# A fixed instruction order in the feed-forward's opening with five plain pairs, and the sample's narrow matmuls of the token mixing moved beside the prompt's

## The chip, the cores and the metric

The kernel runs on one core of one Trainium2 chip. The core has TensorE (matrix multiplies, PE in the profile; its weight loads are PEld), VectorE (DVE), ScalarE (ACT), GpSimd (POOL) and SyncE (SP), which here only issues transfers. The metric is the device time of one launch in microseconds (us), as a median of runs. The profile is one execution recorded by the hardware profiler.

## The reference, cut to what matters

One inference step of a two-layer decoder trunk of width 1024, on a prompt of 512 positions and a sample of 8 sequences with 8 new positions each (64 positions). The kernel treats them together as T = 576 columns. Each layer is:

```
x = x + norm(mixing(norm(x)))       # mixing: three groups of heads beside each other
x = x + norm(conv_ffn(norm(x)))     # d_ff = 2816
mixing: one input projection, then
   A  dilated sliding-window softmax attention, 8 heads of 64
   B  HGRN2 gated linear recurrence, 4 heads, key 128, value 64
   C  GLA linear attention, 4 heads, key 32, value 64
   and one output projection of the joined heads
conv_ffn: up projection to 2 x 2816 columns, causal depthwise convolution of width 3,
   h = gelu(a) * b of the two halves, down projection to 1024
```

The outputs are the two activations, the updated recurrent and convolution states, and the attention's key and value caches, whose old rows are copied from one place of HBM to another.

## The kernel before, in words

Everything is fp32 in value. A factor is split in two parts of a shorter fp32 format (`whi` and `wlo` of a weight, `xha`/`xm` and `xla` of an activation), and a product is the sum of three matmuls: high by high, low by high, high by low (L132 to L134). ScalarE writes the high part (L113) and VectorE the low one (L114). The 576 columns are worked in a half of 320 (the 64 of the sample and 256 of the prompt) and one of 256.

**Token mixing.** The projection's matmuls fill TensorE, and between them stand the small matmuls of the linear-attention heads. For each head and level, the scores are one matmul for the sample (L487, 64 stationary columns) and eight for the prompt (L493), in two PSUM banks. Each fp32 matmul shows in the profile as two. `ke`, the attention's probabilities `pr` and the head outputs' squares `sqs` each have a sample part that is only 64 wide (L529, L954, L721). The head norms take their inverse root on GpSimd (`rsqrt`, L250), once for the prompt's 8 columns (`rh`) and once for the sample's 2 (`rhs`).

**Feed-forward, up projection.** There are 22 pairs of tiles (a and b), j = 0 to 21; tile ui = 2j + i. The first `NPLAIN` pairs are plain: a tile is 8 x 3 matmuls for the half of 320 and 8 x 3 for that of 256 (`col_tile`), and VectorE takes the result out of PSUM into `u` (L1055). The later pairs are fast (`fast_pair`, `products`): seven products of 12 matmuls on 288 columns, a Strassen-like scheme, whose weights need four additions on VectorE and a split of sums (`weights`), and whose activations `sxh`, `sxl` are made once per layer by `combine(0)` to `combine(3)` (L1117 to L1126) on VectorE and ScalarE. These four stand behind tiles 3 to 6. After the two tiles of a pair come `conv_end` (three taps, L1075 on ScalarE, L1076 and L1077 on VectorE) and `h_tile` (gelu L1086, product L1087, split L1097 and L1098). Finished `h` go to the down projection, whose columns `c` are placed after pairs by `FF_AFTER`, in groups of pairs (group 0: pairs 0 to 3).

**What sets the order.** The engines' order in the opening is not written out: a scheduler places instructions by their readiness, with `behind(...)` as bounds. PSUM offers the plain tiles three main banks, so a tile's matmuls wait until VectorE has emptied the bank three halves earlier. SP issues all transfers from one queue in order; after each pair it issues two cache copies (`copy_cache`, 768 KB each, from HBM to HBM).

Of the kernel before, what the change touches and what calls it, by code (L numbers as in the profile page):

```python
# [8 lines left out]
F32 = mybir.dt.float32  # L9
# [30 lines left out]
FF_AFTER = ({4: 2, 5: 2, 6: 2, 7: 2}, {8: 2, 9: 2, 10: 2, 11: 2}, {12: 2, 13: 2, 14: 2, 15: 2},  # L40
# [3 lines left out]
NPLAIN = 4  # L44
COMBINE = (3, 4, 5, 6)
# [34 lines left out]
def trunk_kernel(ctx: ExitStack, tc: tile.TileContext, I, O):  # L80
# [16 lines left out]
    def s_bank():  # L97
        return bank("s", 2)
# [72 lines left out]
    mhalf = cst.tile([P, 8], F32, name="mhalf")  # L171
# [73 lines left out]
    def rsqrt(src, m, scale, name, rows=P):  # L245

        v = rs.tile([P, 8], F32, name="rv", tag="rv", bufs=2)[:rows, :m]
        r = rs.tile([P, 8], F32, name=name, tag=name, bufs=2)[:rows, :m]
# [189 lines left out]
    def gla_tile(l, hp, kq, q, k, b, heads, kd, vt, vs, vcol, s0, o_ps, os_ps, outs, qbd, j, sds, vms, kTs):  # L438
# [58 lines left out]

# [31 lines left out]
        PE.transpose(tb[:TS, :P], ke[:, 0:TS], ident)  # L529
# [56 lines left out]
    def mixing(l, act, first):  # L586
# [16 lines left out]
        with ExitStack() as mx:  # L603
# [63 lines left out]
            with ExitStack() as hx:  # L667
# [40 lines left out]
                def finish(ft):  # L708

                    o, osm = o_holder[ft]  # L710
                    sqt = hp.tile([P, TP], F32, name="sqt", tag="t512", bufs=2)
                    S.activation(sqt, o, AF.Square)
                    sqs = hp.tile([P, TP], F32, name="sqs", tag="t512", bufs=2)
                    S.activation(os_sb[:, ft, :], osm[:, :TS], AF.Copy)
                    S.activation(sqs[:, :TS], osm[:, :TS], AF.Square)
# [15 lines left out]
                    for e in range(2):  # L731
                        mm = PE.matmul(tb[64 * e:64 * e + 64, :TS], rsm[:, e:e + 1].to_broadcast([TS, 64]),
                                       ident[:TS, :TS], start=True, stop=True)
# [79 lines left out]
            G.memset(sTs[TS:, :], 0.0)  # L813
            G.memset(vas[TS:, :], 0.0)

            for p in range(4):
# [121 lines left out]
                pr = sp.tile([P, NEED + TS], F32, name="pr", tag="pr", bufs=1)  # L938
# [18 lines left out]
                V.tensor_copy(sTs[:TS, :], tb[:TS, 256:384])  # L957
# [52 lines left out]
    def ffn(l, y, xpool, act, first):  # L1010
# [20 lines left out]
        with ExitStack() as fx:  # L1031
# [6 lines left out]
            def conv_begin(ui):  # L1038
# [14 lines left out]
                def plain(b, hf, t0, n):  # L1053
                    r = R[:, t0:t0 + n]
                    place(t0, n, lambda d, c: V.tensor_tensor(d, c(b), c(r), ALU.mult))  # L1055
                    if hf:
                        conv_end(ui)
# [7 lines left out]
            def conv_end(ui):  # L1065
                u = us.pop(ui)
                uv = u[:, 0:80].rearrange("p (b t) -> p b t", t=10)
                G.tensor_copy(cso[:, ui, 0:16].rearrange("p (b t) -> p b t", t=2), uv[:, :, 8:10])
                G.tensor_copy(cso[:, ui, 16:18], u[:, NU - 2:NU])  # L1069
                c = cp.tile([P, NU - 2], F32, name="c", tag="c", bufs=2)  # L1070

                def wc(i):
                    o = PR_WC + (l * 2 * NJ + ui) * 3 + i
                    return par[:, o:o + 1]
                S.activation(c, u[:, 0:NU - 2], AF.Copy, scale=wc(0))  # L1075
                V.scalar_tensor_tensor(c, u[:, 1:NU - 1], wc(1), c, ALU.mult, ALU.add)  # L1076
                V.scalar_tensor_tensor(c, u[:, 2:NU], wc(2), c, ALU.mult, ALU.add)  # L1077
                cs[ui] = c
                if ui % 2:
                    h_tile(ui // 2)  # L1080
# [3 lines left out]
            def h_tile(j):  # L1084
                ca, cb = cs.pop(2 * j), cs.pop(2 * j + 1)
                S.activation(ca, ca, AF.Gelu_apprx_tanh)  # L1086
                V.tensor_tensor(cb, ca, cb, ALU.mult)  # L1087
# [3 lines left out]
                for hf, d0, d1, c0, c1 in ((0, 0, TS, 0, 80), (0, TS, 320, 80, 336), (1, 0, 256, 336, NU - 2)):  # L1091
                    src, dh, dl = cb[:, c0:c1], hh[j][hf][:, d0:d1], hl[j][hf][:, d0:d1]
                    if c0 == 0:
                        src = src.rearrange("p (b t) -> p b t", t=10)[:, :, 0:8]
                        dh = dh.rearrange("p (b t) -> p b t", t=8)
                        dl = dl.rearrange("p (b t) -> p b t", t=8)
                    S.activation(dh, src, AF.Copy)  # L1097
                    V.tensor_tensor(dl, src, dh.bitcast(F32), ALU.subtract)  # L1098
# [13 lines left out]
            def combine(i):  # L1112

                with behind(last_lo[0].ins):
                    x1, x2, ua, ta = (y[4 * (i % 2) + m] for m in range(4))
                    for k, d in ((i, x1), (i + HK, x2)):
                        V.scalar_tensor_tensor(d, xt[k], gnorm(l, 2, k), R, ALU.mult, ALU.mult)  # L1117
                    V.tensor_tensor(ua[:, :SH], x1[:, :SH], x1[:, SH:], ALU.subtract)
                    V.scalar_tensor_tensor(ua[:, SH:], x2[:, SH:], -1.0, ua[:, :SH], ALU.mult, ALU.subtract)
                    V.tensor_tensor(ta[:, :SH], x2[:, SH:], x1[:, SH:], ALU.subtract)  # L1120
                    V.scalar_tensor_tensor(ta[:, SH:], ua[:, SH:], -1.0, x2[:, :SH], ALU.mult, ALU.subtract)
                    hi, lo = (cp.tile([P, 7 * SH], F32R, name=f"{n}{i}", tag=f"{n}{i}") for n in ("sxh", "sxl"))
                    for src, m, n in ((x1[:, :SH], B11, 1), (x2, B21, 2), (ua, U1, 2), (ta, T3, 2)):
                        cols = slice(m * SH, (m + n) * SH)
                        S.activation(hi[:, cols], src, AF.Copy)
                        V.tensor_tensor(lo[:, cols], src, hi[:, cols].bitcast(F32), ALU.subtract)  # L1126
                    xs.append((hi, lo))

            def weights(j):
# [11 lines left out]
                w2 = split_w(ws, WN)  # L1141
                w1 = split_w(r1, WN, sw, 2)
                V.tensor_tensor(r0[:, b], r0[:, b], ws[:, a], ALU.add)
                w3 = split_w(r0[:, b], HW)
                return w0, w1, w2, w3

            def fast_pair(j):
                with behind(last_lo[0].ins if j == NPLAIN else None):
                    w0, w1, w2, w3 = weights(j)
                e1, e2 = (conv_begin(2 * j + i)[1] for i in range(2))  # L1150
                with behind(last_mm[0].ins if j == NPLAIN else None):
                    products(w0, w1, w2, w3, e1, e2)
# [32 lines left out]

            def up(j):
                if j >= NPLAIN:
                    fast_pair(j)
                else:
                    for ui in (2 * j, 2 * j + 1):  # L1190
                        if ui >= NFIRST:
                            col_tile(load_w(I["w_up"][l, ui]), xh, xl, allk, conv_begin(ui)[0])
                            if ui in COMBINE:
                                combine(COMBINE.index(ui))
                copy_cache()
                copy_cache()
# [13 lines left out]
            for j in range(NJ + 1):  # L1210
                if j < NJ:
                    up(j)
                    if j == NPLAIN - 1:

                        xpool.release()
                        sw = right_pool(f"sw{l}")
# [231 lines left out]
```

## Time and profile before

| | |
|---|---|
| median of 3 runs | 1683.43 us (1682.94 to 1683.83) |
| profiled execution, and its span | 1681.14 us, 1679.4 us |
| TensorE busy | 1606.9 us, 96% |
| VectorE, ScalarE, GpSimd busy | 1248.1, 877.6, 556.9 us |
| TensorE's granted clock, mean | 0.985 |

The busy shares are means over stages of different kinds. The two layers follow each other; in layer 0 mixing takes the time to about 443 us, the feed-forward's opening is 443 to 515 us, and layer 1 repeats it some 831 us later. The page's 40 slices show TensorE at 9 tenths nearly everywhere, with a dip at the twelfth slice (the opening of layer 0, about 462 to 504 us) and at the thirty-second (the same place of layer 1).

### The profile page before, as it was taken

Reading aid. Unit: us, or ns where it says so; the run is one execution under the profiler, and the core shown is the slowest. Engines: PE = TensorE matmul, PEld = TensorE weight load, DVE = VectorE, ACT = ScalarE, POOL = GpSimd, SP = SyncE. Lnnn points to the kernel's source line nnn. Section 1 sums busy time; section 2 is a strip of 40 time slices with the busy share of each in tenths; the row PEclk is TensorE's granted clock in tenths of the full one; section 3 lists DMA queues with packets and bytes.
Section 4 is the critical chain, followed back from the end, with each engine's and each line's share of the span. In section 5 each row is a group of like instructions: output and inputs, shape, how many; then the busy total and the mean of one; then the engine's idle time right before and its main releaser. Section 6 shows DMA issues by size and latency. Waiting matters only on the chain.

```text
span 1679.4 us, 35933 instructions
## 1 busy us (share of the span) xinstructions
PE 1606.9 (96%) x14256; PEld 1526.1 (91%) x14256; DVE 1248.1 (74%) x2472; ACT 877.6 (52%) x1638; POOL 556.9 (33%) x800
## 2 busy tenths in 40 slices
PE   8999999999979999999989999989999799999997
PEld 7888997789879999999988899968998799999997
DVE  6775765656898888888757757566568978888985
ACT  6754524564556545555456544255735555555541
POOL 4554332302542111221365553332044411212303
PEclk9999999999989999999999999999999899999999
DMA  5221326848424545653522212378474264456432
GB/s 187 71 71 59 103 100 258 298 181 313 142 102 164 212 159 171 220 200 105 174 80 84 78 65 80 120 280 336 159 272 157 82 213 157 171 200 242 149 119 104
DMA packets 74889, 270.36 MB, mean 161 GB/s; under 512 B 10689, under 2 KB 23265, under 8 KB 73185
## 3 DMA queue, kind: packets, MB, share of 16 engines
q1 hardware_dynamic: 74720, 268.07, 45.0%
q8 instruction: 112, 1.84, 0.4%
q14 instruction: 57, 0.46, 0.1%
HBM read 250.11 MB, written 85.02 MB: 200 GB/s over the span
## 4 chain that ended last, share of the span: by engine, by line
PE 76%; DVE 10%; ACT 5%; POOL 3%; issue 3%; DMA 2%; POOLq 0%; SPq 0%; ACTq 0%; DVEq 0%
PE ps_m L132 14%; PE ps_m L134 13%; PE ps_m L133 13%; PE ps_m L1164 4%; PE ps_m L1162 4%; PE ps_m L1163 4%; DVE wlo L114 2%; PE ps_t L1163 2%; PE ps_t L1164 2%; PE ps_t L1162 2%; PE ps_s L493 2%; DMA wraw<-in_w_up 1%; PE ps_o L965 1%; PE ps_o L869 1%; POOL x L352 1%
## 5 line engine op out<-in xcount | busy, mean ns | idle before, releaser
L113 ACT ACTIVATE whi<-wraw 128x1024 fp32r<-128x1024 f32 (+4 forms) x284 | 247.0, 877 | 209.2 <-PE ps_m L133 55.4
L114 DVE TENSOR_TENSOR wlo<-wraw,whi 128x1024 fp32r<-128x1024 f32 (+4 forms) x284 | 285.4, 1010 | 94.6 <-ACT whi L113 88.3
L132 PE MATMUL ps_m<-xha,whi 128*128 128x320 f32 x864 | 272.4, 316 | 5.4 <-ACT whi L113 3.1
L133 PE MATMUL ps_m<-xla,whi 128*128 128x320 f32 x864 | 270.9, 314 | 0.0
L134 PE MATMUL ps_m<-xha,wlo 128*128 128x320 f32 x864 | 268.4, 314 | 0.5 <-DVE wlo L114 0.5
L132 PE MATMUL ps_m<-xm,whi 128*128 128x256 f32 x864 | 248.6, 288 | 18.5 <-DVE u L1055 18.5
L134 PE MATMUL ps_m<-xm,wlo 128*128 128x256 f32 x864 | 247.8, 287 | 0.0
L133 PE MATMUL ps_m<-xm,whi 128*128 128x256 f32 x864 | 246.9, 286 | 0.0
L132 PEld LDWEIGHTS ps_m<-xm,whi 128*128 128x128 f32 x864 | 165.9, 192 | 22.0 <-issue 20.5
L132 PEld LDWEIGHTS ps_m<-xha,whi 128*128 128x128 f32 x864 | 164.1, 190 | 9.5 <-ACT whi L113 4.3
L1162 PE MATMUL ps_m<-sxh,whi 128*128 128x288 f32 x576 | 170.0, 296 | 0.7 <-ACT acc L1168 0.7
L1163 PE MATMUL ps_m<-sxh,wlo 128*128 128x288 f32 x576 | 169.7, 295 | 0.0
L1164 PE MATMUL ps_m<-sxl,whi 128*128 128x288 f32 x576 | 169.7, 295 | 0.0
L133 PEld LDWEIGHTS ps_m<-xm,whi 128*128 128x128 f32 x864 | 166.1, 192 | 1.5 <-issue 1.1
L134 PEld LDWEIGHTS ps_m<-xm,wlo 128*128 128x128 f32 x864 | 166.1, 192 | 1.1 <-issue 0.2
L133 PEld LDWEIGHTS ps_m<-xla,whi 128*128 128x128 f32 x864 | 164.3, 190 | 2.5 <-issue 2.0
L134 PEld LDWEIGHTS ps_m<-xha,wlo 128*128 128x128 f32 x864 | 163.3, 190 | 2.8 <-issue 1.4
L1069 POOL COPY cso<-u 128x2 f32<-128x2 f32 x88 | 74.4, 845 | 268.3 <-DVE u L1180 199.5
L1162 PEld LDWEIGHTS ps_m<-sxh,whi 128*128 128x128 f32 x576 | 108.4, 188 | 1.2 <-ACT acc L1168 1.2
L1163 PEld LDWEIGHTS ps_m<-sxh,wlo 128*128 128x128 f32 x576 | 108.7, 189 | 0.0
L1164 PEld LDWEIGHTS ps_m<-sxl,whi 128*128 128x128 f32 x576 | 108.3, 188 | 0.0
L1041 POOL COPY u<-cso 128x16 f32<-128x16 f32 x88 | 59.8, 682 | 136.7 <-DVE c L1077 86.9
(342 smaller groups left out, 4187.6 us busy)
## 6 DMA issues: line engine op xcount, KB each, us to landing
wraw<-in_w_up SPq DMA_DIRECT2D x88, 512.0 KB, 3.8
kv<-in_ck SPq DMA_DIRECT2D x32, 768.0 KB, 6.6
kv<-in_cv SPq DMA_DIRECT2D x32, 768.0 KB, 7.0
out_ck<-in_ck SPq DMA_DIRECT2D x32, 768.0 KB, 7.7
out_cv<-in_cv SPq DMA_DIRECT2D x32, 768.0 KB, 6.8
wraw<-in_w_s SPq DMA_DIRECT2D x42, 512.0 KB, 3.6
wraw<-in_w_dn SPq DMA_DIRECT2D x48, 256.0 KB, 2.6
x<-xdr SPq DMA_DIRECT2D x24, 288.0 KB, 6.4
```

Of the source, the lines that this page charges most:

```text
L113: S.activation(hi[:, :n], raw[:, :n], AF.Copy)
L114: last_lo[0] = V.tensor_tensor(lo[:, :n], raw[:, :n], hi[:, :n].bitcast(F32), ALU.subtract)
L132: PE.matmul(out, ah, bh, start=(i == 0), stop=False)
L133: PE.matmul(out, ah, bl, start=False, stop=False)
L134: last_mm[0] = PE.matmul(out, al, bh, start=False, stop=(i == n - 1))
L352: (V if dram_out and k % 4 == 3 else G).tensor_tensor(xk, xk, yk, ALU.add)
L493: mm = PE.matmul(bp[64 * hh:64 * hh + 64, cp * nh * 32:(cp + 1) * nh * 32], xk[:, c0:c0 + 64], moving(c0), start=True, stop=True)
L1041: G.tensor_copy(uv[:, :, 0:2], cso[:, ui, 0:16].rearrange("p (b t) -> p b t", t=2))
L1069: G.tensor_copy(cso[:, ui, 16:18], u[:, NU - 2:NU])
L1162: PE.matmul(b, wh, xh, start=i == 0 and not more, stop=False, skip_group_check=more)
L1163: PE.matmul(b, wl, xh, start=False, stop=False, skip_group_check=more)
L1164: PE.matmul(b, wh, xl, start=False, stop=i == HK - 1, skip_group_check=more)
```

## The change

Two independent parts.

*Token mixing.* For heads with one group (`nh == 1`) the sample's score matmul writes columns 128 to 159 of the prompt's PSUM bank, directly ahead of the prompt's eight, and its masked copy follows the prompt's. The transposes of `ke` and of `pr` for the sample take 128 columns instead of 64. `finish` squares prompt and sample into one tile and makes five sum matmuls and one inverse root of 10 columns, instead of four and one, with roots of 8 and 2. `pr` becomes a tile of the layer with a zeroed tail.

*Feed-forward's opening.* `NPLAIN` is 5 instead of 4, so pair 4 is two plain tiles. `opening()` writes out the order of VectorE, ScalarE and GpSimd for tiles 3 to 9 under `manual_schedule`: norms, combinations, low parts, taps, convolution sums, gelu, splits, evacuations (`ev`) and weights, with the weights of pair 5 made early. The column groups of the down projection's group 0 follow pairs 5, 6 and 7 (2, 3 and 3) instead of pairs 4 to 7 (2 each). Ten cache copies, which stood two after each pair, are all issued after the opening, and the two of pair 5 follow without a weight load between.

```diff
-FF_AFTER = ({4: 2, 5: 2, 6: 2, 7: 2}, ...
+FF_AFTER = ({5: 2, 6: 3, 7: 3}, ...
-NPLAIN = 4
-COMBINE = (3, 4, 5, 6)
+NPLAIN = 5
...
+            bp = s_bank()
             if sample:
-                bs = s_bank()
-                PE.matmul(bs[:TS, :nh * 32], xk[:, 0:TS], moving(0), start=True, stop=True)
-                level_scores(B, lv, sds[:TS], bs[:TS, :nh * 32])
-            bp = s_bank()
+                bs = bp[:TS, 128:160] if nh == 1 else s_bank()[:TS, :nh * 32]
+                PE.matmul(bs, xk[:, 0:TS], moving(0), start=True, stop=True)
+                if nh > 1:
+                    level_scores(B, lv, sds[:TS], bs)
...
             level_scores(B, lv, sdm, bp[:, :128 * nh])
+            if sample and nh == 1:
+                level_scores(B, lv, sds[:TS], bs)
...
-        PE.transpose(tb[:TS, :P], ke[:, 0:TS], ident)
+        PE.transpose(tb[:, :P], ke[:, 0:P], ident)
...
-                    for i in range(4):
-                        PE.matmul(tb[:, 2 * i:2 * i + 2], sqt[:, i * P:(i + 1) * P], blk2, start=True, stop=True)
-                    r = rsqrt(tb[:, :8], 8, 1.0, "rh")
-                    tb = t_bank()
-                    mark(f"f{ft}.a", PE.matmul(tb[:TS, :2], sqs[:, :TS], blk2, start=True, stop=True))
-                    rsm = rsqrt(tb[:TS, :2], 2, 1.0, "rhs", TS)
+                    for i, c0 in enumerate((0, P, 2 * P, 3 * P, T - P)):
+                        mm = PE.matmul(tb[:, 2 * i:2 * i + 2], sq[:, c0:c0 + P], blk2, start=True, stop=True)
+                    mark(f"f{ft}.a", mm)
+                    r = rsqrt(tb[:, :10], 10, 1.0, "rh")
...
-                mm = PE.transpose(tb[:TS, 256:384], pr[:, 768:832], ident)
+                mm = PE.transpose(tb[:, 256:384], prs[:, NEED:], ident)
...
+                def ev(*keys):
+                    for key in keys:
+                        if key[1] == 0:
+                            evs[key[0]] = conv_begin(key[0])[0]
+                        evs[key[0]](*bs.pop(key))
+                        if halves:
+                            mm()
...
+                with tc.manual_schedule(engines=ORDERED):
...
+                    ev((4, 0))
+                    load(6)
+                    c.append(normalize(1))
+                    combine(1, *c[1])
+                    taps(2, 3)
+                    ev((4, 1))
+                    conv_sums(2, 3)
+                    h_gelu(1)
+                    ev((5, 0))
+                    lows(1, c[1][0])
+                    load(7)
+                    ev((5, 1), (6, 0))
...
+                    ev((8, 1), (9, 0))
+                    w = weights(NPLAIN)
+                    next(w)
+                    ev((9, 1))
+                    h_split(2)
+                    early[NPLAIN] = next(w)
+                for ui in range(6, 2 * NPLAIN):
+                    conv_end(ui)
+                for _ in range(2 * NPLAIN):
+                    copy_cache()
```

VectorE's queue in layer 0 before, around the evacuation that ends the long wait; `L1055 u` is the evacuation of PSUM, `L1126 sxl` a low part of the combined activations, `L1076` and `L1077` the convolution sums, `L114 wlo` the low part of a weight, L1140 an addition for a fast weight.

```order
L1076 SCALAR_TENSOR_TENSOR c<-u,par,c 128x592
L1126 TENSOR_TENSOR sxl_6067<-y_4688,sxh_6066 128x576
L1077 SCALAR_TENSOR_TENSOR c<-u,par,c 128x592
L1120 TENSOR_TENSOR y_4690<-y_4688,y_4687 128x288
L114 TENSOR_TENSOR wlo<-wraw,whi 128x1024
L1119 SCALAR_TENSOR_TENSOR y_4689<-y_4688,y_4689 128x288
L1121 SCALAR_TENSOR_TENSOR y_4686<-y_4685,y_4684 128x288
L114 TENSOR_TENSOR wlo<-wraw,whi 128x1024
L1126 TENSOR_TENSOR sxl_5981<-y_4685,sxh_5980 128x576
L1077 SCALAR_TENSOR_TENSOR c<-u,par,c 128x592
L114 TENSOR_TENSOR wlo<-ws,whi 128x1024
L1055 TENSOR_TENSOR u<-ps_m,rbc 128x8x8
```

The same queue after, a stretch of `opening()`; `L1059 u` is now the evacuation, L1139 the norm, L1146 to L1149 the combination, L1093 the convolution sums and L1156 the low parts.

```order
L1139 SCALAR_TENSOR_TENSOR y_4649<-x_4922,par,rbc 128x576
L1146 TENSOR_TENSOR y_4650<-y_4648 128x288
L1147 TENSOR_TENSOR y_4651<-y_4649,y_4648 128x288
L1148 SCALAR_TENSOR_TENSOR y_4650<-y_4649,y_4650 128x288
L1149 SCALAR_TENSOR_TENSOR y_4651<-y_4650,y_4649 128x288
L1059 TENSOR_TENSOR u<-ps_m,rbc 128x256
L1093 SCALAR_TENSOR_TENSOR c<-u,par,c 128x592 x4
L1059 TENSOR_TENSOR u<-ps_m,rbc 128x8x8
L1059 TENSOR_TENSOR u<-ps_m,rbc 128x256
L1156 TENSOR_TENSOR sxl_5873<-y_4648,sxh_5872 128x288
L1156 TENSOR_TENSOR sxl_5873<-y_4649,sxh_5872 128x576
```

Evacuations stand at most some ten instructions apart, where twenty stood between two of them before (L1055 at places 636 and 658 of the queue).

TensorE's queue in the mixing of layer 0, before: one sample matmul (L487) alone between projection matmuls.

```order
L132 MATMUL ps_m<-xm_149,whi 128x256
L133 MATMUL ps_m<-xm_149,whi 128x256
L134 MATMUL ps_m<-xm_149,wlo 128x256
L487 MATMUL ps_s<-lev 64x32
L132 MATMUL ps_m<-xm_152,whi 128x256
L133 MATMUL ps_m<-xm_152,whi 128x256
```

After, the sample's matmul (now L488) directly ahead of the prompt's eight (now L494).

```order
L132 MATMUL ps_m<-xm_158,whi 128x256
L488 MATMUL ps_s<-lev 64x32
L494 MATMUL ps_s<-lev 64x32 x8
L488 MATMUL ps_s<-lev 64x32
L494 MATMUL ps_s<-lev 64x32 x8
L529 MATMUL ps_t<-con,ke 128x128 x4
```

No sample matmul of a single group stands alone any more; over both layers 13 did.

SP's queue of layer 0's opening before, in which pairs of copies stand between the weight loads.

```order
L120 DMA wraw<-in_w_up 128x1024 x2
L1029 DMA out_ck<-in_ck 16x12288 x2
L1134 DMA wraw<-in_w_up 128x1024 x2
L1029 DMA out_ck<-in_ck 16x12288 x2
L120 DMA wraw<-in_w_dn 128x512 x2
L1134 DMA wraw<-in_w_up 128x1024 x2
```

After, from tile 6's weights on.

```order
L119 DMA wraw<-in_w_up 128x1024 x4
L1163 DMA wraw<-in_w_up 128x1024 x2
L1033 DMA out_ck<-in_ck 16x12288 x12
L119 DMA wraw<-in_w_dn 128x512 x2
L1163 DMA wraw<-in_w_up 128x1024 x2
L1033 DMA out_ck<-in_ck 16x12288 x2
```

Twelve copies stand in one piece ahead of the first two loads of the down projection's weights (`w_dn`).

## Rows read from the trace of the kernel before

**Rows 1.** Two windows: busy us (instructions) of PE, PEld, DVE, ACT, POOL; clock; DMA.

```profile
440.00:480.00 40.00, 32.93 (x243) 32.05 (x241) 38.11 (x71) 22.84 (x34) 14.21 (x18) 0.98 0.39 139
480.00:520.00 40.00, 34.41 (x243) 33.77 (x244) 37.59 (x67) 23.39 (x48) 16.69 (x25) 0.89 0.43 151
```

**Rows 2.** TensorE's waits in the two layers' openings: total us, times, longest.

```profile
PE ps_m L132 <- DVE u L1055: 9.9, 2, 9.6
...
PE ps_m L132 <- DVE u L1055: 8.6, 1, 8.6
```

**Rows 3.** Timeline of TensorE at the stall: start, duration, instruction, [wait, releaser].

```profile
484.95 0.55 PE L132 MATMUL ps_m<-xm,whi 128*128 128x256 f32 x1 [9.58 <-DVE u L1055]
...
485.52 0.41 PE L134 MATMUL ps_m<-xm,wlo 128*128 128x256 f32 x1
485.73 0.41 PE L132 MATMUL ps_m<-xm,whi 128*128 128x256 f32 x1
```

**Rows 4.** Timeline of TensorE in the mixing: narrow matmuls alone and in company.

```profile
61.19 0.31 PE L134 MATMUL ps_m<-xha,wlo 128*128 128x320 f32 x1
61.43 0.30 PE L487 MATMUL ps_s<-lev 128*64 128x32 f32 x2
61.66 0.42 PE L132 MATMUL ps_m<-xha,whi 128*128 128x320 f32 x1
61.92 0.31 PE L133 MATMUL ps_m<-xla,whi 128*128 128x320 f32 x1
...
63.57 1.12 PE L493 MATMUL ps_s<-lev 128*64 128x32 f32 x32
...
65.12 0.27 PE L529 MATMUL ps_t<-con,ke 128*64 128x128 f32 x1
65.15 0.36 PE L133 MATMUL ps_m<-xm,whi 128*128 128x256 f32 x1
65.35 0.28 PE L134 MATMUL ps_m<-xm,wlo 128*128 128x256 f32 x1
```

**Rows 5.** Timeline of TensorE, matmuls at full pace.

```profile
601.33 0.31 PE L132 MATMUL ps_m<-xha,whi 128*128 128x320 f32 x1
601.48 0.31 PE L133 MATMUL ps_m<-xla,whi 128*128 128x320 f32 x1
601.62 0.28 PE L132 MATMUL ps_m<-xm,whi 128*128 128x256 f32 x1
601.74 0.28 PE L133 MATMUL ps_m<-xm,whi 128*128 128x256 f32 x1
```

**Rows 6.** Timeline of VectorE through the opening.

```profile
443.67 3.50 DVE L114 TENSOR_TENSOR wlo<-wraw,whi 128x1024 fp32r<-128x1024 f32 x3
...
475.57 0.68 DVE L1140 TENSOR_TENSOR ws<-wraw 128x512 f32<-128x512 f32 x1
476.17 0.82 DVE L1076 SCALAR_TENSOR_TENSOR c<-u,par,c 128x592 f32<-128x592 f32 x1
...
488.05 0.55 DVE L1055 TENSOR_TENSOR u<-ps_m,rbc 128x64 f32<-128x64 f32 x2
488.51 0.68 DVE L114 TENSOR_TENSOR wlo<-wraw,whi 128x512 fp32r<-128x512 f32 x1
...
506.35 1.23 DVE L114 TENSOR_TENSOR wlo<-wraw,whi 128x1024 fp32r<-128x1024 f32 x1 [0.16 <-ACT whi L113]
```

**Rows 7.** Timeline of ScalarE in the opening.

```profile
458.45 1.06 ACT L113 ACTIVATE whi<-wraw 128x1024 fp32r<-128x1024 f32 x1 [4.47 <-issue]
...
466.20 0.77 ACT L1075 ACTIVATE c<-u,par 128x592 f32<-128x592 f32 x1
466.88 0.67 ACT L1125 ACTIVATE sxh<-y 128x576 fp32r<-128x576 f32 x1
```

**Rows 8.** Landing of the copies issued at 446.4 and 447.0, and the load at 447.7.

```profile
DMA to landing us min/median/max: 6.8/7.4/8.0
...
DMA to landing us min/median/max: 8.6/8.6/8.6
```

More of the change, by code (lines that the diff above doesn't have):

```diff
@@ L1065, in conv_end @@
             def conv_end(ui):
[L1066 to L1074, printed above, removed]
@@ L1110, in ffn @@
             xs, sw = [], None
[L1112 to L1127, printed above, removed]
@@ new lines, in normalize, with combine @@
+            def normalize(i):
+                x1, x2, ua, ta = (y[4 * (i % 2) + m] for m in range(4))
+                for k, d in ((i, x1), (i + HK, x2)):
+                    V.scalar_tensor_tensor(d, xt[k], gnorm(l, 2, k), R, ALU.mult, ALU.mult)
+                xs.append([cp.tile([P, 7 * SH], F32R, name=f"{n}{i}", tag=f"{n}{i}") for n in ("sxh", "sxl")])
+                return ((x1[:, :SH], B11, 1), (x2, B21, 2), (ua, U1, 2), (ta, T3, 2)), (x1, x2, ua, ta)
+            def combine(i, parts, tiles):
+                x1, x2, ua, ta = tiles
+                V.tensor_tensor(ua[:, :SH], x1[:, :SH], x1[:, SH:], ALU.subtract)
+                V.tensor_tensor(ta[:, :SH], x2[:, SH:], x1[:, SH:], ALU.subtract)
+                V.scalar_tensor_tensor(ua[:, SH:], x2[:, SH:], -1.0, ua[:, :SH], ALU.mult, ALU.subtract)
+                V.scalar_tensor_tensor(ta[:, SH:], ua[:, SH:], -1.0, x2[:, :SH], ALU.mult, ALU.subtract)
+                for src, m, n in parts:
+                    S.activation(xs[i][0][:, m * SH:(m + n) * SH], src, AF.Copy)
@@ L1129, in weights, with lows @@
+            def lows(i, parts):
+                for src, m, n in parts:
+                    cols = slice(m * SH, (m + n) * SH)
+                    V.tensor_tensor(xs[i][1][:, cols], src, xs[i][0][:, cols].bitcast(F32), ALU.subtract)
             def weights(j):
@@ L1144, in weights @@
                 w3 = split_w(r0[:, b], HW)
-                return w0, w1, w2, w3
+                yield w0, w1, w2, w3
             def fast_pair(j):
-                with behind(last_lo[0].ins if j == NPLAIN else None):
-                    w0, w1, w2, w3 = weights(j)
-                e1, e2 = (conv_begin(2 * j + i)[1] for i in range(2))
+                w = early.pop(j, None)
+                if w is None:
+                    *_, w = weights(j)
                 with behind(last_mm[0].ins if j == NPLAIN else None):
-                    products(w0, w1, w2, w3, e1, e2)
+                    products(*w, *(conv_begin(2 * j + i)[1] for i in range(2)))
             def products(w0, w1, w2, w3, e1, e2):
@@ L1184, in products @@
                 e2(0, lambda d, c: S.activation(d, c(ba), AF.Copy, scale=-1.0), True)
-            def up(j):
[L1187 to L1194, printed above, removed]
+            early = {}
@@ new lines, in opening, with load, mm @@
+            def opening():
+                nonlocal xpool, sw
+                ws, bs, evs = {}, {}, {}
+                halves = [(ui, hf) for ui in range(NFIRST, 2 * NPLAIN) for hf in range(2)]
+                def load(*uis):
+                    for ui in uis:
+                        ws[ui] = load_w(I["w_up"][l, ui])
+                def mm():
+                    ui, hf = halves.pop(0)
+                    col_half(ws[ui], xh, xl, allk, hf, lambda *a: bs.__setitem__((ui, hf), a))
+                def ev(*keys):
[6 more added lines that the diff above has]
+                with tc.manual_schedule(engines=ORDERED):
+                    load(3, 4, 5)
+                    c = [normalize(0)]
+                    taps(0, 1)
+                    for _ in range(3):
+                        mm()
+                    conv_sums(0, 1)
+                    h_gelu(0)
+                    ev((3, 0))
+                    combine(0, *c[0])
+                    lows(0, c[0][0])
+                    h_mult(0)
+                    ev((3, 1))
+                    h_split(0)
+                    ev((4, 0))
[10 more added lines that the diff above has]
+                    ev((5, 1), (6, 0))
+                    h_mult(1)
+                    c.append(normalize(2))
+                    combine(2, *c[2])
+                    h_split(1)
+                    load(8)
+                    ev((6, 1))
+                    lows(2, c[2][0])
+                    taps(4, 5)
+                    ev((7, 0))
+                    load(9)
+                    ev((7, 1))
+                    conv_sums(4, 5)
+                    h_gelu(2)
+                    c.append(normalize(3))
+                    combine(3, *c[3])
+                    xpool.release()
+                    sw = right_pool(f"sw{l}")
+                    ev((8, 0))
+                    lows(3, c[3][0])
+                    h_mult(2)
+                    ev((8, 1), (9, 0))
[8 more added lines that the diff above has]
+                    copy_cache()
@@ L1209, in ffn @@
             first_tiles(first, act, [conv_begin(i)[0] for i in range(NFIRST)])
-            for j in range(NJ + 1):
+            opening()
+            for j in range(NPLAIN, NJ + 1):
                 if j < NJ:
                     up(j)
-                    if j == NPLAIN - 1:
-                        xpool.release()
-                        sw = right_pool(f"sw{l}")
                 else:
```

88 lines of the change are left out of this document (57 added, 31 removed).

## The prediction

> **What bounds the kernel now.** I read the page's 40 slices first: TensorE stands at 9 tenths everywhere except in the slices of the two feed-forward openings, so a change elsewhere has to shorten TensorE's own queue to count. The windows of layer 0's opening say who holds it back [rows 1]: TensorE is busy 32.93 + 34.41 = 67.3 of 80 us while VectorE, busy 75.7 of 80, is the full engine; ScalarE has 34 us free. The list of waits puts TensorE's idle time there on one cause, the evacuation of PSUM to `u` by VectorE: 9.9 us in layer 0 and 8.6 us in layer 1 [rows 2]. The timeline shows one piece of it, 9.58 us until 484.95, and behind it matmuls of 256 columns 0.21 us apart [rows 3] where 0.12 is usual [rows 5]; some sixteen of them at that half rate (the 1.2 GHz level) cost another 1.6 us. VectorE is not slow at the evacuation: it stands in its queue behind twenty other instructions, as the order shows. I take the opening as bound by VectorE's sum of work, the rest of both layers as bound by TensorE.
>
> **The mixing, part by part.** A lone sample matmul costs more than its work. Between the 320-column matmul at 61.19 and the next at 61.66 lie 0.47 us, and from there to 61.92 another 0.26, in place of 0.15 each [rows 4, 5], that is 0.43 us for the sample's two passes. In a run of 32 such passes one takes 1.12 / 32 = 0.035 us [rows 4], so two in company cost 0.07. Moving one beside the prompt's saves 0.36 us; 13 stood alone by the order, 13 x 0.36 = 4.7 us over both layers. The ten narrow transposes of `ke` have a smaller price: from 65.15 to 65.35 are 0.20 us instead of 0.12 [rows 4], so 0.08 each. The eight of `pr` are of the same kind, and I give the eight pairs of sums for the narrow squares the same, since the fifth wide sum takes back part of what the switch cost: 26 x 0.08 = 2.1 us at most; I take two thirds, 1.4, because a widened one streams or loads somewhat more. The single inverse root of ten columns replaces two on GpSimd, which has spare time, and I cost it at nothing: its cover is the projection's matmuls behind each head; without that cover it would give back the second root's time, a gain that I leave out. Together -6.1 us. The bounds: 3 us if at half of the places another wait (a score's mask on VectorE, one bank instead of two) ends last instead, and 4.7 + 26 x 0.11 = 7.6 us if every one of the 26 costs what the slow step behind the sample's matmul costs beyond its usual pace.
>
> The Trainium skill ("TensorEngine Tiling (Array Packing)", Key Properties) says that a change of the tiling mode drains TensorE; the lone matmuls of 128*64 between those of 128*128 are such changes, and the trace agrees for the score matmul with 0.36 us. By that rule the 26 others pay a whole drain too, which is the second rival below; the 0.08 us row speaks against it.
>
> **The opening, part by part.** Per layer, pair 4 as a plain pair is 48 matmuls of 320 and 48 of 256 columns instead of 84 of 288. By starts 0.15, 0.12 and (288 columns, in proportion) 0.135 us apart [rows 5]: 7.2 + 5.8 - 11.3 = +1.7 us on TensorE. For VectorE it drops the fast weights, three splits of 1024 at 3.50 / 3 = 1.14 (start to start, with the overlap off), one of 512 at 0.60 and four additions of 512 at 0.60 [rows 6], 3.4 + 0.6 + 2.4 = 6.4 us, and brings two plain splits, 2.3 us, and 0.4 us more evacuation (1152 columns instead of 864 by VectorE; a tile's 320 columns take 0.46) [rows 6]: -3.7 us. All else is the same work in another order.
>
> Before, VectorE does not pause from 443.67 until 506.35, where it waits 0.16 us [rows 6]. So a different order cannot remove idle time of VectorE; it can only choose who gets served first, and take work out. If VectorE stays full, the opening ends 3.7 us earlier, and TensorE's added 1.7 us lie inside the 10 us that it idles. But the written order is kept literally on ScalarE too, and there I find four places where VectorE must stand behind it. The sums of tiles 2 and 3 need their first tap, which ScalarE starts only after the four high parts of the second combination: after VectorE's last step of the combination a high part of 0.6 and a tap of 0.7 us [rows 7] plus a hand-over, with one evacuation of VectorE in between: 1.4 us. The split of the second `h` stands behind the four high parts of the third combination: again 1.4. The low part of tile 8's weight follows its high part, 1.0 us [rows 7], with 0.4 covered: 0.6. The sum weight of pair 5 needs a high part that can start only after its addition: 0.9. That makes 4.3 us in which VectorE, and the evacuations queued behind, are later. -3.7 + 4.3 = +0.6 us per layer, +1.2 over both. The long stall goes, and what is late next are many waits of under 2.5 us: each half of tiles 6 to 9, and the products of pair 5 that wait for its low parts. What bounds this from both sides: none of the four waits occurs (-3.7 per layer), or they delay TensorE with a half-rate spell each time instead of once (+4.3 - 3.7 + 3 x 1.6, about +5 per layer).
>
> Moving the cache copies is free as long as the loads behind them land in time. A copy issued at 446.44 landed 6.8 us later, the next, issued at 447.0, 8.0 us later, and a load behind both, issued at 447.68, 8.6 us later [rows 8]: 453.2, 455.0 and 456.3. I take the 1.8 us between the copies as the rate. Twelve in one piece from about 484 us (my reckoning of when the loads of pair 5 have found buffers) land from 490.8 to 490.8 + 11 x 1.8 = 510.6, and the first load of the down projection's weights about 1.3 behind, 511.9. Counting both queues forward, I find it wanted at about 511, with a pair's matmuls on TensorE to cover a delay of a microsecond or two: 0 us, with a bound of +5 per layer.
>
> **Sum.** -6.1 + 1.2 = -4.9 us from the profiled execution's 1681.14: 1676.2. The median of the runs is 2.3 above that execution, so I forecast 1678.5.
>
> **Rivals.**
> - *VectorE stays full.* If ScalarE, which is free 34 us of 80, keeps ahead, the opening gains 3.7 per layer, and without a 9 us gap TensorE's clock does not fall, 1.6 more in each: 7.4 + 3.2 = 10.6, with the mixing 16.7: 1666.7. For it: rows 1. Against it: ScalarE's order is now fixed as written. The Trainium skill ("TensorE: Matmul & The Clock Gate", Part 1) says that the clock follows how busy the array has lately been; by that rule short waits spread out would hold the clock, and the trace agrees so far as the fall stands behind the long gap.
> - *Every change of width costs a whole drain.* Then the mixing saves 39 x 0.36 = 14.0 and the sum is -12.8: 1670.6. Against it: the transposes' 0.08.
> - *The copies hold back the down projection's weights.* The loads stand behind twelve copies in one queue; if the copies start at 488 or take 2.2 us each, the first load lands at 516, 5 us after it is wanted. VectorE and ScalarE stop at its split, in whose queues stand the evacuations of pair 6, so TensorE loses it whole: +10 over both layers, less 4.9: 1688.5. It decides from 4.2 us of lateness per layer. For it: SP's order and the load that took 8.6 us behind only two copies. Against it: by my count they are just in time.
> - *The mixing gives nothing*, because the next wait ends last at the same places: 1683.4 + 1.2 = 1684.6. For it: one bank now carries both score blocks. Against it: TensorE is nearly gapless there.
> - *Short waits with half-rate spells* in the opening, +5 per layer: -6.1 + 10 = +3.9, 1687.3.
>
> **How the numbers follow.** My forecast has 0.42, VectorE full 0.20, whole drains 0.08, late copies 0.12, no mixing gain 0.09, half-rate spells 0.09. About 0.2%, 3.4 us, is what a measurement of this kernel can tell from no change. The forecast's own range, 1673 to 1684, is faster by that in 0.27 of its 0.42, the same in 0.13; it leaves 0.02 for slower. The first two rivals are faster, 0.28; the fourth is the same, 0.07 of 0.09; late copies and spells are slower, 0.19 of 0.21. Faster 0.55, same 0.22, slower 0.23. The range reaches to the first and third rival, 1664 to 1689.
>
> **What would show it.** In the mixing: no lone pass at the sample's matmul, its two passes directly in front of the prompt's at 0.035 us each, and the time from the start to the out-projection shorter by about 3 us per layer. In the opening: no wait of TensorE for `u` above 2.5 us; VectorE's waits for ScalarE 4 us per layer in four places; window sums of VectorE 3.7 us lower. If those waits are absent, the first rival is right; if TensorE or VectorE waits for the load of `w_dn` around 511 us, the third. The prediction is wrong if the opening changes by more than 4 us per layer either way, or if the mixing's gain is under 3 us.

## The result, and the profile after

The changed kernel takes 1700.2 us (median of 4 runs, 1692.86 to 1704.05) beside 1683.18 us for the kernel before on the same chip: a ratio of 1.009 with an interval of 1.0063 to 1.0118, so 11 to 20 us slower. The forecast was 1678.5 us with a range of 1664 to 1689. The profiled execution took 1699.44 us.

I cut both traces at the same places of the program: a layer's mixing is from the last matmul of its norm to the first sum of the norm behind it, its feed-forward from the norm ahead of it to the next layer's norm. The windows give length, TensorE's busy time (count), then PEld, VectorE, ScalarE, GpSimd, the granted clock, DMA share and GB/s. The kernel before, mixing of layers 0 and 1, then feed-forward of layers 0 and 1:

```profile
30.59:404.55 373.96, 362.34 (x3852) 325.91 (x3852) 238.69 (x552) 197.44 (x354) 133.97 (x149) 0.99 0.44 158
861.47:1235.38 373.91, 360.62 (x3852) 325.11 (x3852) 234.91 (x552) 195.33 (x352) 138.06 (x151) 0.99 0.44 158
...
443.30:822.01 378.71, 365.81 (x2711) 362.96 (x2710) 328.82 (x556) 204.93 (x380) 84.99 (x169) 0.99 0.50 175
1274.43:1653.94 379.51, 368.07 (x2711) 365.33 (x2710) 325.51 (x553) 202.29 (x377) 86.93 (x169) 0.98 0.48 167
```

The same four stretches of the changed kernel:

```profile
32.09:405.92 373.83, 358.75 (x3853) 324.76 (x3852) 237.71 (x548) 192.93 (x351) 135.11 (x145) 0.99 0.43 152
867.13:1249.55 382.42, 363.26 (x3852) 329.00 (x3852) 236.22 (x548) 195.48 (x352) 137.88 (x147) 0.97 0.42 149
...
444.78:827.59 382.81, 368.81 (x2722) 364.87 (x2721) 325.84 (x552) 201.99 (x373) 72.72 (x173) 1.00 0.54 185
1288.93:1672.10 383.17, 370.68 (x2723) 366.48 (x2722) 322.67 (x549) 199.16 (x370) 74.33 (x173) 0.99 0.52 178
```

So the mixing stayed as long in layer 0 (-0.1 us) and grew by 8.5 us in layer 1; the feed-forward grew by 4.1 and 3.7 us. In layer 0's mixing TensorE is busy 3.6 us less, where about 3 was forecast, and idles 3.5 us more (length less busy time, 11.6 and 15.1 us); a part of the 3.6 is the clock, as experiment 8 shows. Both feed-forwards have 3 us less work on VectorE, and are longer all the same.

In the opening the long stall of [rows 2, 3] is gone. TensorE's waits in the feed-forward of layer 0, then of layer 1 (total, times, longest):

```profile
PE ps_m L131 <- ACT whi L112: 3.8, 2, 3.5
PE ps_m L131 <- DVE u L1059: 3.8, 4, 1.7
...
PE ps_m L131 <- ACT whi L112: 2.8, 1, 2.8
PE ps_m L131 <- DVE u L1059: 2.3, 2, 1.7
```

The evacuation costs 3.8 and 2.3 us in waits of at most 1.7, where it cost 9.9 and 8.6. New is a wait for the high part of a weight. ScalarE's timeline in layer 0 says what that waited for:

```profile
510.96 0.77 ACT L1087 ACTIVATE c<-u,par 128x592 f32<-128x592 f32 x1
516.02 0.63 ACT L112 ACTIVATE whi<-wraw 128x512 fp32r<-128x512 f32 x1 [4.29 <-DMA wraw<-in_w_dn]
```

The weight is the first of the down projection. SP's queue, with the time from issue to landing of the twelve copies and of those two loads by line:

```profile
473.97 8.63 SPq L1163 DMA_DIRECT2D wraw<-in_w_up  x2
482.65 13.76 SPq L1033 DMA_DIRECT2D out_ck<-in_ck  x12
498.22 8.74 SPq L119 DMA_DIRECT2D wraw<-in_w_dn  x2
...
DMA to landing us min/median/max: 6.3/15.5/19.1
...
DMA to landing us min/median/max: 10.1/13.9/17.8
```

The load issued at 498.22 lands 17.8 us later, at 516.0, behind copies that took up to 19.1 us; I had put it at 511.9. The first copy landed at 488.9 and the last, issued at 495.90, 18.8 us later at 514.7: one every 2.3 us. VectorE stops 3.54 us at the same weight, and so does TensorE:

```profile
516.69 0.69 DVE L113 TENSOR_TENSOR wlo<-wraw,whi 128x512 fp32r<-128x512 f32 x1 [3.54 <-ACT whi L112]
516.71 0.63 PE L131 MATMUL ps_m<-xha,whi 128*128 128x320 f32 x1 [3.54 <-ACT whi L112]
```

VectorE's four waits for ScalarE in the opening, which the prediction counted at 1.4, 1.4, 0.6 and 0.9 us, are all there:

```profile
466.89 3.07 DVE L1093 SCALAR_TENSOR_TENSOR c<-u,par,c 128x592 f32<-128x592 f32 x4 [1.18 <-ACT c L1087]
479.46 0.73 DVE L1121 TENSOR_TENSOR xla<-c,xha 128x64 fp32r<-128x64 f32 x2 [0.98 <-ACT xha L1119]
481.02 1.23 DVE L113 TENSOR_TENSOR wlo<-wraw,whi 128x1024 fp32r<-128x1024 f32 x1 [0.49 <-ACT whi L112]
...
502.80 1.23 DVE L113 TENSOR_TENSOR wlo<-ws,whi 128x1024 fp32r<-128x1024 f32 x1 [0.75 <-ACT whi L112]
```

In the mixing the joined matmuls do what they should. TensorE's timeline, the sample's two passes (L488) among the prompt's (L494):

```profile
81.31 0.24 PE L488 MATMUL ps_s<-lev 128*64 128x32 f32 x1 [0.46 <-DVE lev L428]
81.33 0.24 PE L494 MATMUL ps_s<-lev 128*64 128x32 f32 x1
81.39 0.22 PE L488 MATMUL ps_s<-lev 128*64 128x32 f32 x1
81.41 0.68 PE L494 MATMUL ps_s<-lev 128*64 128x32 f32 x15
82.01 0.42 PE L133 MATMUL ps_m<-xha,wlo 128*128 128x320 f32 x1
```

Eighteen passes take 0.70 us, 0.039 each, near the 0.035 in company in [rows 4]; but the group waits 0.46 us for its level first. Layer 1's worst place is a wait of 3.35 us for VectorE's four level products (`work`), which here take 4.83 us while GpSimd computes `q` and then `vm`. VectorE, GpSimd and TensorE:

```profile
1054.44 4.83 DVE L434 TENSOR_TENSOR work<-lev,work 32x256 f32<-32x256 f32 x4
...
1055.07 2.73 POOL L858 TENSOR_TENSOR q<-qp,q 64x512 fp32r<-64x512 f32 x2
1057.88 2.29 POOL L550 TENSOR_TENSOR vm<-vbs,bmask 64x512 f32<-64x512 f32 x2
...
1059.41 1.97 PE L494 MATMUL ps_s<-work,lev 128*64 128x128 f32 x16 [3.35 <-DVE work L434]
```

In the kernel before the same four products stand beside `vm` but not beside `q`, and take 2.82 us; TensorE has no wait for `work` there.

```profile
1040.93 2.82 DVE L435 TENSOR_TENSOR work<-lev,work 32x256 f32<-32x256 f32 x4
...
1042.26 2.38 POOL L547 TENSOR_TENSOR vm<-vbs,bmask 64x512 f32<-64x512 f32 x2 [0.43 <-PE ps_t L549]
```

### The profile page after: what moved, and what is told of

It is laid out like the page before. It is cut to its first block, busy times and chain, and to the rows that moved or that the text cites. A ratio compares the mean times of both kernels' runs of the same rounds, so it can differ in the third digit from the quotient of the medians.

```text
span 1697.6 us, 35902 instructions
## 1 busy us (share of the span) xinstructions
PE 1611.1 (95%) x14280; PEld 1530.7 (90%) x14280; DVE 1242.6 (73%) x2456; ACT 867.3 (51%) x1622; POOL 531.0 (31%) x792
## 5 line engine op out<-in xcount | busy, mean ns | idle before, releaser
L131 PE MATMUL ps_m<-xha,whi 128*128 128x320 f32 x896 | 283.8, 317 | 14.5 <-ACT whi L112 8.7
L133 PE MATMUL ps_m<-xha,wlo 128*128 128x320 f32 x896 | 280.1, 315 | 1.3 <-DVE wlo L113 1.3
L132 PE MATMUL ps_m<-xla,whi 128*128 128x320 f32 x896 | 281.0, 314 | 0.0
L131 PE MATMUL ps_m<-xm,whi 128*128 128x256 f32 x896 | 255.9, 286 | 2.0 <-DVE u L1059 2.0
L132 PE MATMUL ps_m<-xm,whi 128*128 128x256 f32 x896 | 255.8, 285 | 0.0
L131 PEld LDWEIGHTS ps_m<-xm,whi 128*128 128x128 f32 x896 | 170.8, 191 | 4.2 <-PE ps_m L133 2.7
L132 PEld LDWEIGHTS ps_m<-xm,whi 128*128 128x128 f32 x896 | 170.9, 191 | 1.9 <-issue 1.3
L1193 PE MATMUL ps_m<-sxh,wlo 128*128 128x288 f32 x544 | 161.6, 297 | 4.1 <-DVE wlo L113 4.1
L1192 PE MATMUL ps_m<-sxh,whi 128*128 128x288 f32 x544 | 160.9, 296 | 3.3 <-ACT whi L112 2.4
L1194 PE MATMUL ps_m<-sxl,whi 128*128 128x288 f32 x544 | 161.0, 297 | 0.0
L1093 DVE SCALAR_TENSOR_TENSOR c<-u,par,c 128x592 f32<-128x592 f32 x176 | 144.3, 829 | 5.5 <-ACT c L1087 4.6
L1085 POOL COPY cso<-u 128x2 f32<-128x2 f32 x88 | 50.3, 571 | 260.7 <-DVE u L1210 173.1
```

The source lines that it names most:

```text
L131: PE.matmul(out, ah, bh, start=(i == 0), stop=False)
L132: PE.matmul(out, ah, bl, start=False, stop=False)
L133: last_mm[0] = PE.matmul(out, al, bh, start=False, stop=(i == n - 1))
L1093: V.scalar_tensor_tensor(c, us[ui][:, i:NU - 2 + i], tap_weight(ui, i), c, ALU.mult, ALU.add)
L1192: PE.matmul(b, wh, xh, start=i == 0 and not more, stop=False, skip_group_check=more)
L1193: PE.matmul(b, wl, xh, start=False, stop=False, skip_group_check=more)
```

## The experiments

All ran on one core beside the kernel before, whose median was 1685.15 us beside experiments 1 to 4, 1684.91 beside 5 to 8 and 1684.01 beside 9 to 11. The ratios are to it, with an interval of 95%; experiments of different groups are compared here by their distance from the kernel before of their own group.

**1. The mixing's edits alone** (the whole diff of the mixing, `NPLAIN` and the opening as before).

> Before with the mixing's edits alone; the feed-forward's opening as before. Theory 1 (the mixing's own edits lose the time in layer 1: by the two profiles layer 0's mixing changed by -0.1 us and layer 1's by +8.5): about 1683.2 + 8.4 = 1691.6, with waits for DVE's level products again around the last heads of layer 1. Theory 2 (layer 1's mixing was disturbed by the opening's changes ahead of it, and the edits themselves are neutral or gain 3 per layer): 1677 to 1683.

Measured: 1691.71 us, ratio 1.0033 (1.0023 to 1.0044). Theory 1 holds: the mixing's edits lose 6.6 us by the medians, 3.9 to 7.4 by the interval, without any change in the opening. The profile has layer 1's mixing at 381.1 us, with the same wait of 3.3 us for `work`, and four products of 4.83 us again; layer 0's at 375.5. The windows of the two mixings:

```profile
30.31:405.77 375.46, 358.85 (x3853) 324.79 (x3852) 237.48 (x548) 192.98 (x351) 135.60 (x145) 0.99 0.44 158
863.61:1244.71 381.10, 361.67 (x3852) 327.54 (x3852) 238.17 (x548) 195.51 (x352) 137.75 (x147) 0.98 0.43 155
```

TensorE idles 16.6 and 19.4 us in them.

**2. The opening's edits alone** (the mixing as before; TensorE's order in it stayed that of before).

> Before with the opening's edits alone; the instruction order in both mixings is that of before. Theory 1: the opening costs what the profiles show from its start to the final phase, +4.1 in layer 0 and +3.7 in layer 1, so 1683.2 + 7.8 = 1691.0. Theory 2 (the opening also spoils layer 1's mixing): 1699 or more.

Measured: 1694.78 us, ratio 1.0049 (1.0032 to 1.0065): +9.6 by the medians, a little more than the 7.8 expected. Layer 1's mixing took 373.88 us as before, so theory 2 falls. The two parts add: 6.6 + 9.6 = 16.2, and the changed kernel lost 17.0.

**3. The opening alone, copies later.**

```diff
-                for _ in range(2 * NPLAIN):
-                    copy_cache()
...
                 copy_cache()
                 copy_cache()
+                if 8 <= j < 14:
+                    copy_cache()
```

> The opening alone, with the ten cache copies behind it moved: two after each pair from pair 5 on, three after pairs 8 to 13. Theory 1 (the wait of 3.5 and 2.8 us for the down projection's first weights is the copies' doing): the wait is gone and the time is 1691.0 - 6.3 = 1684.7. Rival (the loads are late for another reason, buffers or SP's own waits, or VectorE is late there anyway and the wait only changes its name): 1690 to 1692, with the same length of TensorE's idle time around the first down columns.

Measured: 1683.94 us, ratio 0.9991 (0.9978 to 1.0003). Layer 0's mixing has the order of before, layer 1's another. The load of the down projection's first weight is issued at 489.49 and lands 5.3 us later; the wait for the down projection's weight is gone, and with it 10.8 us beside experiment 2, more than the 6.3 of the two waits. TensorE's waits in layer 0's feed-forward, of this kernel:

```profile
PE ps_m L131 <- DVE u L1054: 3.8, 4, 1.7
PE ps_m L1188 <- DVE wlo L113: 2.1, 2, 1.2
PE ps_t L275 <- POOL rr L249: 1.3, 1, 1.3
PE ps_m L1187 <- ACT whi L112: 1.2, 1, 1.2
```

What is left are short waits for VectorE and ScalarE and, as before, the norm's root on GpSimd. The surplus of 4.5 us over the two waits can be followed in the profiles of experiments 2 and 3. In experiment 2's own trace the waits were longer, 4.1 and 3.4 us. Layer 0's feed-forward shortens from 385.42 to 377.24 us, of which 5.5 are TensorE's idle time, and layer 1's from 384.82 to 381.37, of which 2.9; the other 3.2 are busy time, with a granted clock of 1.00 instead of 0.99 in layer 0. The edit also moved some of TensorE's matmuls in the feed-forward, and what that alone is worth was not tested.

**4. Both parts, copies later** (the same edit on the changed kernel).

> The changed kernel with the copies moved as in the run before; the program's order in layer 1's mixing is another one than in the changed kernel, since the scheduler places it anew. Theory 1: 1700.2 - 6.3 = 1693.9, if layer 1's mixing stays 8 us long of before whatever its order. Rival (that loss hangs on one unlucky order in layer 1): 1685 to 1688.

Measured: 1685.95 us, ratio 1.0002 (0.9991 to 1.0012). The rival holds: layer 1's mixing, placed in another order, took 377.6 instead of 382.4 us, which is still 3.7 more than before. Beside experiment 3 the mixing's edits now cost 2.0 us, not 6.6.

**5. The score join alone** (sample's matmul in the prompt's bank, its masked copy last).

> Of the mixing's edits the score join alone: the sample's score matmul in the prompt's bank and directly ahead of it, its masked copy last. Theory A (the loss of the mixing, +6.6 us with all its edits, comes from this edit: TensorE no longer takes the sample's block early, and comes to the joined block before VectorE has the level's product): +5 to +8 us, with waits of TensorE at L494 for DVE lev longer than before's. Theory B (the transposes, the joined squares and the single root put the order out): 0 to -4 us.

Measured: 1688.47 us, ratio 1.002 (1.0009 to 1.0032): +3.6, half of the mixing's loss, and in neither theory's range. This time layer 0 (381.05 us, at a clock of 0.97) has the bad meeting and layer 1 (373.4 us) has none. VectorE, GpSimd and TensorE of this kernel in layer 0:

```profile
212.61 4.82 DVE L435 TENSOR_TENSOR work<-lev,work 32x256 f32<-32x256 f32 x4
...
213.23 2.73 POOL L858 TENSOR_TENSOR q<-qp,q 64x512 fp32r<-64x512 f32 x2
...
217.57 1.97 PE L495 MATMUL ps_s<-work,lev 128*64 128x128 f32 x16 [3.77 <-DVE work L435]
```

**6. The widths and the single root alone** (the mixing's other edits).

> The mixing's other edits alone: transposes of ke and pr of 128 columns, squares in one tile, five sums, one root of ten columns; the score matmuls as before. Theory A: -1 to -2 us (26 changes of width at 0.08 us or a little less). Theory B: +5 to +8.

Measured: 1688.94 us, ratio 1.0015 (1.0 to 1.003), +4.0 by the medians and 0 to +5 by the interval, so no gain either: neither theory's number. With the 3.6 of experiment 5 it makes 7.6, beside 6.6 for all the edits. Layer 0's mixing has the idle time of before plus 0.9 us (12.5) but a busy TensorE of 364.3 instead of 362.3 at a clock of 0.98. The interval reaches to 1.0; what the widths cost or give is not settled by it.

**7. The opening alone, copies later, ScalarE's work for a waiting VectorE first.**

```diff
                     c.append(normalize(1))
-                    combine(1, *c[1])
                     taps(2, 3)
+                    combine(1, *c[1])
...
                     c.append(normalize(2))
-                    combine(2, *c[2])
                     h_split(1)
                     load(8)
+                    combine(2, *c[2])
```

> The opening alone with the copies later, and three moves in its written order: the taps of tiles 2 and 3 ahead of the second combination, and the split of the second h and tile 8's weight ahead of the third. If VectorE's waits for ScalarE cost TensorE their length (the prediction's step, 1.18 + 0.98 + 0.49 us in layer 0 of the changed kernel), those three are gone and the time is 2 x 2.6 = 5 us below the opening with the copies later, so about 1679. Rival (VectorE's lost time is covered, since the waits that TensorE has there end on the evacuation's place in the queue, and the moves delay the evacuations by as much): within 1.5 us of it.

Measured: 1679.34 us, ratio 0.9967 (0.9953 to 0.9982), 5.6 us below the kernel before where experiment 3 is 1.2 below: 4.4 us won, where 5 were expected. This is a version faster than both kernels. Only the last of the four waits is left on VectorE, and TensorE has none for the evacuation; VectorE's wait and the longest of TensorE's list for layer 0's feed-forward:

```profile
499.14 1.23 DVE L113 TENSOR_TENSOR wlo<-ws,whi 128x1024 fp32r<-128x1024 f32 x1 [1.41 <-ACT whi L112]
...
PE ps_t L1188 <- DVE wlo L113: 2.2, 1, 2.2
PE ps_m L1188 <- DVE wlo L113: 2.1, 2, 1.2
PE ps_m L1187 <- ACT whi L112: 1.5, 1, 1.5
```

The three waits of 2.65 us are gone, but the last one and TensorE's wait for `wlo` have grown (1.41 and 2.2 us, in experiment 3 at most 1.1 and 0.4). In layer 0's opening VectorE's waits for ScalarE fall from 3.8 us in all to 1.4, and TensorE's idle time in the feed-forward from 9.4 to 7.7, with the same order of its matmuls (in layer 1 from 9.4 to 7.8). So most of VectorE's lost time is TensorE's, not all of it. Layer 0's feed-forward of experiments 3 and 7:

```profile
447.68:824.92 377.24, 367.83 (x2722) 364.59 (x2721) 325.50 (x552) 202.08 (x373) 73.38 (x173) 1.00 0.53 188
```

```profile
443.86:820.38 376.52, 368.79 (x2722) 365.90 (x2721) 325.17 (x552) 201.72 (x373) 73.54 (x173) 0.99 0.53 188
```

**8. The score join with a bank of its own for the sample** (`bs = s_bank()[:TS, :nh * 32]`, the order of the code as in experiment 5).

> As the score join, but the sample's block keeps a PSUM bank of its own. If the shared bank is what costs (one bank's two readers, or the bank released later), the time is that of before or up to 4 us below. If the place of the sample's matmul and of its masked copy in the order is what costs, it is as long as the score join.

Measured: 1684.62 us, ratio 0.9997 (0.9982 to 1.0012). The experiment does not answer its question: with a bank of its own the scheduler puts the sample's matmul back where it stood, and the orders of TensorE and VectorE are those of the kernel before, instruction by instruction. So it shows that matmuls written beside each other are not placed beside each other, and that the 3.6 us of experiment 5 come with the shared bank and the order that follows from it. Which of the two costs them is not shown. As a second measurement of the same order it also gives the mixings of before at another granted clock:

```profile
30.23:402.94 372.71, 361.00 (x3852) 324.46 (x3852) 238.74 (x552) 197.58 (x354) 134.18 (x148) 0.99 0.44 159
861.87:1235.48 373.61, 359.58 (x3852) 324.28 (x3853) 233.96 (x552) 196.11 (x352) 137.73 (x151) 1.00 0.44 158
```

Layer 0's TensorE is busy 1.3 us less than in the profile of the kernel before with the same instructions: the clock is 0.991 here and 0.986 there. The changed kernel's 358.75 us and experiment 1's 358.85 were taken at 0.991, so the edits of the mixing save 2.2 us in this layer, not 3.6.

**9. The mixing's edits alone, with q's low part of the first head pair on VectorE.**

```diff
-                    G.tensor_tensor(q2[o_, hb, :], qp[r, :], q2[r, hb, :].bitcast(F32), ALU.subtract)
+                    (V if p == 0 else G).tensor_tensor(q2[o_, hb, :], qp[r, :], q2[r, hb, :].bitcast(F32), ALU.subtract)
```

> The mixing's edits alone, with one operation of the first head pair moved from GpSimd to VectorE (the low part of q, L858, 64x512 twice), which in the mixing-alone run stood beside VectorE's four level products and these took 4.8 us instead of 1.8. Theory C (that meeting makes TensorE's longest wait, 3.3 us in one layer): the products take 1.8 us again, that wait is gone, and the time is some 3 to 5 us below the mixing alone, 1687 to 1689. Rival (the wait is the order's, whatever the products take): within 1.5 us of 1691.7.

Measured: 1688.33 us, ratio 1.002 (1.0009 to 1.003), 4.3 us above the kernel before where experiment 1 is 6.6 above: 2.2 us won, less than expected, and the two intervals overlap. VectorE's products in layer 1 took 3.04 us instead of 4.83, and TensorE's wait for them fell by as much, from 3.3 to 1.5 us:

```profile
1048.68 3.04 DVE L435 TENSOR_TENSOR work<-lev,work 32x256 f32<-32x256 f32 x4
...
PE ps_s L495 <- DVE work L435: 1.5, 1, 1.5
```

They still met another operation of GpSimd (`vm`, at 1050.39), as they do in the kernel before, where they take 2.82 us; the 1.8 us of the expectation belong to other products of the same line, which nothing meets. So `q` makes 1.8 us of the wait. The rest of it, 1.5 us, TensorE does not have in the kernel before; it goes with the order that the mixing's edits brought. With the move the scheduler placed both mixings in yet another order, and TensorE idles 1.2 us less in layer 1 and 1.6 less in layer 0, where the products did not meet `q` before either.

**10. The kernel before with the same move**, as control.

> The kernel before with the same move, as a control: there the products do not meet that operation, so Theory C expects no gain, between -1 and +1.5 us (VectorE has 1.3 us more work per layer where TensorE does not wait for it).

Measured: 1684.86 us, ratio 1.0002 (0.9987 to 1.0016): nothing, as expected. That fits a gain that needs the meeting, but the gain of experiment 9 is too small to prove it by the times.

**11. The changed kernel with the copies later and the opening's order of experiment 7.**

> The changed kernel with the copies later and the three moves in the opening's order. If the parts add, it is the repaired opening alone (1679.3) plus what the mixing's edits cost beside it (+2.0 between the two runs with the copies later): 1681. If the mixing's cost returns as in the mixing alone, 1686.

Measured: 1681.7 us, ratio 0.9982 (0.997 to 0.9994). It is 2.3 us below the kernel before, where experiment 7 is 5.6 below. The parts add to within the noise: with the opening mended the changed kernel is a little faster than before, and by the medians it would be faster still without the mixing's edits, though the intervals of experiments 7 and 11 overlap.

## Why the prediction was wrong

By the experiments the forecast of 1678.5 us was off in three terms: the copies, put at 0, cost 10.8 us; the mixing, put at -6.1, cost 6.6; the opening, put at +1.2, gained 1.2. That makes 1699.6, and 1700.2 were measured.

*What bounds the kernel* was right: the opening is VectorE's, and experiment 7 shows that most of what VectorE waits there TensorE loses (2 x 2.65 us of waits gone, 4.4 us won).

*The opening's own sum*, +1.2 us, was near: without the copies' effect the opening measures -1.2 us (experiment 3, by its interval -3.7 to +0.5). The four waits were found at the right places and summed to 3.4 us instead of 4.3; VectorE's work fell by 3.0 instead of 3.7.

*The step that failed first* is "Moving the cache copies is free as long as the loads behind them land in time ... 0 us, with a bound of +5 per layer". The mechanism was there as the third rival with its price, +10 for both layers, and experiment 3 measures 10.8; what I had wrong is the rate. I took the 1.8 us between two copies, but the twelve landed 2.3 us apart, so that the last came at 514.7 instead of 510.6 although the first was issued at 482.65 and not, as reckoned, at 484. The load behind them landed at 516.0, the time that the rival named for a load 5 us late. I gave that case 0.12.

*The step that failed second* is the mixing's -6.1 us, which took saved work for saved time and put TensorE's waits at nothing. The saved work is real but smaller than forecast: 2.2 us in layer 0 at the same clock (experiments 1 and 8), against 3.05 per layer (10 of the 13 lone matmuls stood in layer 0, so that the prediction's own prices give 10 x 0.36 + 0.7 = 4.3 there); in layer 1 the clocks, 0.98 and 1.00, do not allow the comparison. The waits grew: TensorE's idle time is 16.6 and 19.4 us in experiment 1 and 11.7 and 14.0 in experiment 8, 10.3 us more over both layers. If layer 1 saves as much work as layer 0, 10.3 less 2 x 2.2 is 5.9 us (an estimate), beside 6.6 measured. The fourth rival said that the next wait ends last at the same places; it expected 0, and 6.6 us were lost. That TensorE is nearly gapless in the mixing was no protection: its order interleaves score matmuls with projection matmuls so that VectorE's levels are just in time, and the edits gave it another order, in which they are not. The whole loss is shown to be the mixing's own (experiments 1 and 2). Of the one long wait of 3.3 to 3.8 us, 1.8 come from GpSimd's `q` beside VectorE's products (experiment 9). The remaining idle time, some 7 us of shorter waits, for `lev`, `ke` and `kT` among others, is only read from the waits, not tested.

The rival of whole drains has no support in layer 0's 2.2 us, where it would save 7 per layer, and the first rival, VectorE full, is what experiment 7 comes near to once the copies are gone: 5.6 us below the kernel before, where the rival's 3.7 per layer would give 7.4 without its share of the clock.

## What to carry to other kernels

Transfers that no engine waits for still have a place in a queue: before moving them, ask which load stands behind them, and take the landing time of the last of the whole burst, not the spacing of two. In an order that was written by hand, work on a second engine that the bound engine needs next belongs ahead of work that it needs later; three such moves gave 4.4 us. Work saved on the busiest engine inside a finely interleaved stage is not yet time: compare its idle time in the same stretch before and after.

## What the runs showed of the hardware that was not expected

VectorE's four products on 32 partitions of 256 columns take 1.75 us when GpSimd stands still (at 1048.28 in the kernel before), 2.82 us beside the end of GpSimd's `lev` and its `vm` (two operations of 64x512), and 4.82 to 4.83 us beside the end of `lev`, its `q` (two subtractions of 64x512) and the start of `vm`, in three kernels (the changed one, experiments 1 and 5).

TensorE's clock changes a stage's time with the same instructions and the same idle time. Layer 0's mixing took 374.0 us in the kernel before and 378.2 us in the profile of experiment 3, whose order of instructions is the same in that stage; the windows of before and of experiment 3 from 31 us on show busy times of 361.43 and 365.41 us at clocks of 0.99 and 0.97:

```profile
31.00:404.00 373.00, 361.43 (x3847) 325.18 (x3847) 238.00 (x551) 197.03 (x353) 133.56 (x147) 0.99 0.44 158
```

```profile
31.00:408.00 377.00, 365.41 (x3844) 328.86 (x3845) 239.45 (x550) 196.72 (x353) 132.95 (x148) 0.97 0.43 151
```

That is why one profile of each kernel was not enough to compare stages by less than 4 us, and why the verdicts above rest on the medians of the runs.
